# One layer's first adaLN modulation on four column tiles of the matmul engine, with the first group's r and k streamed after the opening

## The chip, the cores and the metric

The kernel runs on one core of a Trainium2 chip. A core has TensorE (PE, matmuls; PEld is its weight load), VectorE (DVE), ScalarE (ACT), GpSimd (POOL) and SyncE (SP), whose queue issues all the transfers here. The metric is the time of one execution on the device in microseconds; less is better.

## The reference, cut to what matters

Two layers of a decoder with 256 tokens and width 2048, all in fp32. Each layer modulates its input by six vectors made from one conditioning vector, projects it, runs two head groups, and then a SwiGLU.

```python
cond = jax.nn.silu(c)
for l in range(DEPTH):
    mod = (jnp.einsum('bd,de->be', cond, w_ada[l]) + b_ada[l]).reshape(B, N_MOD, 1, D_MODEL)
    sh_m, sc_m, gt_m, sh_f, sc_f, gt_f = [mod[:, i] for i in range(N_MOD)]
    u = x * (1 + sc_m) + sh_m
    proj = u @ w_in[l]
    ...   # sliding-window attention on q, k, v; RWKV-7 on r, k, v and the lora columns
    mix = jnp.concatenate([y_attn, y_rwkv], axis=-1) @ w_out[l]
    x = layer_norm(DEEPNORM_ALPHA * x + gt_m * mix, ln1_w[l], ln1_b[l])
    u = x * (1 + sc_f) + sh_f
    gate, up = jnp.split(u @ w_gate_up[l], 2, axis=-1)
    ffn = (jax.nn.silu(gate) * up) @ w_down[l]
    x = layer_norm(DEEPNORM_ALPHA * x + gt_f * ffn, ln2_w[l], ln2_b[l])
```

`w_ada[l]` is 2048 x 12288, so the two modulations that the first `u` needs (shift and scale, columns 0 to 4095 of layer 0) are 33.5 MB of weights for a product with a single row.

## The kernel before, in words

Weights stream from memory in raw tiles (`steps`): ScalarE rounds a tile to fp32r (`hi`, L380), VectorE takes the rest (`lo`, L381), and TensorE makes three fp32r products of each block (hi with u's high half, hi with its low half, lo with the high half; L414 to L416 in `tstream`, where u is the moving operand with 256 columns, L402 to L405 in `stream`). There are four raw tiles, three of hi and two of lo.

The opening is the part up to the first mixer. It goes over the 16 blocks of 128 columns of u in five parts of 4, 4, 2, 4 and 2 blocks (`PARTS`). For each part `ada_first` loads the weights of both modulations, 16 blocks of 128 rows, into tiles `ast`; VectorE multiplies each by its element of `cond` and adds it to `aacc` (L304, L306), which leaves one partial sum for each partition. `ada_sums` transposes the 128x128 blocks of `aacc` on TensorE (L277), ScalarE adds up along the free axis while it reads (L281), and VectorE adds the bias (L284). Then `make_u` transposes x (L354) and writes u's blocks (ScalarE L358, L360, VectorE L361). With every part of u that is ready, `front` runs three streams of columns: the 288 lora columns (`lb`), the 1024 of V (`acc`), and, with `ahead`, 384 columns of r and k: both r blocks and the first k block of group 0 (`rk`, and a third of it in `lb`). They accumulate in PSUM over all parts. A block of u takes 9 lora products, 9 of r and k, and 24 of V, and 42 in all.

The mixer works through groups in a fixed order (`ORDER`: D0 R0 A0 D1 R1 I0 ...). D0 makes the decays from the lora columns (products zb and ab, then vt from V), R0 (`project(0)`) streams the one k block that is left, A0 (`prepare`) mixes r and k with the token before (`shift_mix`, ScalarE and VectorE) and makes the chunk matrices, whose inversion I0 starts on TensorE at L749, after a round trip through memory and GpSimd.

The order on each engine is not that of the code: a scheduler sets it at build time from its own estimates. Each engine then works in that order and waits for semaphores. In PSUM the opening has bank m0 for all small work (transposes) and bank m1 for `rk`.

The remaining modulations run later, one load and one VectorE sum at a time beside the weight streams (`ada_steps`, L257).

## Time and profile before

| | us |
|---|---|
| time, median of 3 runs (lowest, highest) | 2701.08 (2698.25, 2703.82) |
| span of the profiled execution | 2692.6 |
| its granted TensorE clock, mean | 0.965 of full |
| TensorE busy over the span | 2501.1 |
| VectorE busy | 1841.0 |
| ScalarE busy | 1188.3 |
| first lora product of part 4 | 141.0 |
| last product of the opening's V stream | 177.3 |
| first product of R0 | 184.5 |

The profiled execution has no time of its own beside its span; the 8.5 us between its span and the runs' median stand for what lies around a span. A row of the profile gives the line, the engine, the operation, out<-in by the program's names, the shapes, and for groups the count, the busy time with the mean in ns, and the idle time ahead with what ended it. Rows of the timeline begin with the start and the length in us. Matmuls are pipelined: the distance of two starts is their price, not the length of one. An fp32 product stands in the trace as two passes, each with a weight load.

### The profile page before, as it was taken

The numbers are of one execution on the slowest core, as the hardware profiler recorded it, in microseconds if no ns is written. First come the engines' busy times: TensorE is split into PE (matmuls) and PEld (weight loads), VectorE is DVE, ScalarE is ACT, GpSimd is POOL, SyncE is SP. The second block draws the span as 40 slices with busy tenths as digits, with TensorE's granted clock in tenths as the row PEclk, the third lists the DMA queues.
The fourth block names the chain that finished last, engine by engine and source line by source line (L and its number), as shares of the span: only waits on it lengthen the run. The fifth ranks groups of instructions, "written<-read, shape, count | busy, mean of one in ns | idle before, by whom it ended". The sixth has DMA issues, their size and how long they took to land.

```text
span 2692.6 us, 41752 instructions
## 1 busy us (share of the span) xinstructions
PE 2501.1 (93%) x15325; PEld 2093.1 (78%) x15325; DVE 1841.0 (68%) x2469; ACT 1188.3 (44%) x2029; POOL 135.0 (5%) x355
## 2 busy tenths in 40 slices
PE   3788998788999999999999999979899999999997
PEld 2687886567888888888889877867688888888887
DVE  6866767979877777777788677555764545545456
ACT  2364452435444444444445544534444444344442
POOL 1002112000000000000000022110000000000000
PEclk9789998899999999999999999989999999999999
DMA  9968668688998888889878586424756656666654
GB/s 315 381 188 253 198 191 238 180 317 296 353 330 309 297 303 312 293 295 308 308 263 304 174 259 188 117 72 144 253 172 188 190 186 196 195 189 189 193 188 149
DMA packets 351999, 637.49 MB, mean 237 GB/s; under 512 B 75894, under 2 KB 142898, under 8 KB 350258
## 3 DMA queue, kind: packets, MB, share of 16 engines
q1 hardware_dynamic: 351794, 634.82, 71.6%
q8 instruction: 120, 1.97, 0.3%
q14 instruction: 85, 0.70, 0.1%
HBM read 622.08 MB, written 12.62 MB: 236 GB/s over the span
## 4 chain that ended last, share of the span: by engine, by line
PE 68%; DMA 8%; DVE 6%; ACT 2%; issue 1%; POOL 1%; SPq 0%; DVEq 0%; POOLq 0%; ACTq 0%
PE acc L403 19%; PE acc L402 19%; PE acc L405 19%; DMA ast<-in_w_ada_dram 3%; DVE aacc L257 2%; PE acc L414 2%; PE acc L415 2%; PE acc L416 2%; DVE lo L381 1%; DMA raw<-in_w_gate_up_dram 1%; PE mb L1225 1%; DMA raw<-in_w_out_dram 1%; DMA yf<-yd 1%; PE mb L277 1%; ACT pr L947 0%
## 5 line engine op out<-in xcount | busy, mean ns | idle before, releaser
L380 ACT CAST hi<-raw 128x1024 fp32r<-128x1024 f32 (+2 forms) x728 | 758.5, 1044 | 1110.8 <-PE acc L405 833.1
L381 DVE TENSOR_TENSOR lo<-raw,hi 128x1024 fp32r<-128x1024 f32 (+2 forms) x728 | 880.2, 1212 | 519.8 <-PE acc L403 347.1
L403 PE MATMUL acc<-lo,u 128*128 128x512 f32 x1568 | 513.4, 395 | 11.9 <-DVE lo L381 11.8
L405 PE MATMUL acc<-hi,u 128*128 128x512 f32 x1568 | 505.8, 391 | 0.0
L257 DVE SCALAR_TENSOR_TENSOR aacc<-ast,cond,aacc 128x1024 f32<-128x1024 f32 x300 | 384.1, 1280 | 127.8 <-DMA ast<-in_w_ada_dram 126.6
L402 PE MATMUL acc<-hi,u 128*128 128x512 f32 x1568 | 457.2, 393 | 0.9 <-ACT u L360 0.5
L403 PEld LDWEIGHTS acc<-lo,u 128*128 128x128 f32 x1568 | 293.8, 189 | 76.4 <-DVE lo L381 16.2
L402 PEld LDWEIGHTS acc<-hi,u 128*128 128x128 f32 x1568 | 294.9, 188 | 63.4 <-ACT sg L1218 0.9
L405 PEld LDWEIGHTS acc<-hi,u 128*128 128x128 f32 x1568 | 295.2, 188 | 61.8 <-issue 0.5
L403 PE MATMUL acc<-lo,ht 128*128 128x512 f32 (+1 forms) x720 | 243.6, 377 | 3.0 <-DVE lo L381 2.9
L405 PE MATMUL acc<-hi,ht 128*128 128x512 f32 (+1 forms) x720 | 242.2, 375 | 0.0
L414 PE MATMUL acc<-u,hi 128*128 128x256 f32 x720 | 206.1, 293 | 14.0 <-ACT hi L380 14.0
L402 PE MATMUL acc<-hi,ht 128*128 128x512 f32 (+1 forms) x720 | 217.0, 376 | 0.0
L415 PE MATMUL acc<-u,hi 128*128 128x256 f32 x720 | 204.5, 291 | 0.0
L416 PE MATMUL acc<-u,lo 128*128 128x256 f32 x720 | 193.1, 294 | 7.1 <-DVE lo L381 7.1
L403 PEld LDWEIGHTS acc<-lo,ht 128*128 128x128 f32 x720 | 135.0, 188 | 29.3 <-DVE lo L381 5.6
L414 PEld LDWEIGHTS acc<-u,hi 128*128 128x128 f32 x720 | 141.9, 197 | 19.3 <-ACT hi L380 14.9
L405 PEld LDWEIGHTS acc<-hi,ht 128*128 128x128 f32 x720 | 135.6, 188 | 24.2
L402 PEld LDWEIGHTS acc<-hi,ht 128*128 128x128 f32 x720 | 134.8, 188 | 24.4
L415 PEld LDWEIGHTS acc<-u,hi 128*128 128x128 f32 x720 | 141.7, 197 | 2.6 <-issue 1.6
L416 PEld LDWEIGHTS acc<-u,lo 128*128 128x128 f32 x720 | 133.8, 197 | 11.6 <-DVE lo L381 9.0
L1067 POOL TENSOR_TENSOR brs<-brs,mhalf 128x1 f32<-128x1 f32 x8 | 7.6, 955 | 1698.7 <-DVE brs L1066 772.1
(349 smaller groups left out, 2901.1 us busy)
## 6 DMA issues: line engine op xcount, KB each, us to landing
ast<-in_w_ada_dram SPq DMA_DIRECT2D x368, 512.0 KB
raw<-in_w_gate_up_dram SPq DMA_DIRECT2D x704, 256.0 KB
raw<-in_w_down_dram SPq DMA_DIRECT2D x176, 512.0 KB
raw<-in_w_in_dram SPq DMA_DIRECT2D x82, 512.0 KB
raw<-in_w_out_dram SPq DMA_DIRECT2D x64, 512.0 KB
raw<-in_w_in_dram SPq DMA_DIRECT2D x120, 256.0 KB
ast<-in_w_ada_dram SPq DMA_DIRECT2D x32, 256.0 KB
lnw<-in_ln_w_dram SPq DMA_DIRECT2D x4, 1024.0 KB
```

The source lines that it names most:

```text
L257: ins = V.scalar_tensor_tensor(acc, t, cond[:, j:j + 1], acc, ALU.mult, ALU.add)
L277: PE.transpose(b[:, i * P:(i + 1) * P], blocks[q + i], ident)
L380: S.copy(h, fl)
L381: ins = V.tensor_tensor(r, fl, h.bitcast(F32), ALU.subtract)
L402: PE.matmul(bt, lhsT=xh, rhs=hi[:, c0:c0 + w], start=st, stop=False)
L403: PE.matmul(bt, lhsT=xh, rhs=lo[:, c0:c0 + w], start=False, stop=False)
L405: PE.matmul(banks[t][q][:, 0:w], lhsT=xl, rhs=hi[:, c0:c0 + w], start=False, stop=sp_)
L414: PE.matmul(bt, lhsT=hi[:, c0:c0 + w], rhs=xh, start=st and opens, stop=False)
L415: PE.matmul(bt, lhsT=hi[:, c0:c0 + w], rhs=xl, start=False, stop=False)
L416: PE.matmul(bt, lhsT=lo[:, c0:c0 + w], rhs=xh, start=False, stop=sp_ and closes)
L1067: G.tensor_tensor(rs[:, 0:1], rs[:, 0:1], mhalf[:, 0:1], ALU.pow)
L1225: PE.transpose(b[:, i * T + t * P:i * T + (t + 1) * P], hh[t][:, (2 * k2 + i) * P:(2 * k2 + i + 1) * P], ident)
```

## The change

`ada_first` keeps its loads, but the product with `cond` is made by TensorE: for each block of 128 rows four fp32 products, one for each half of the two modulations' columns, on the four column tiles of 32 columns (`gv[32q:32q+32]`). The stationary operand is the element of `cond`, repeated 32 times, and the weights are the moving operand. They accumulate over the 16 row blocks in bank m1. ScalarE copies the result, TensorE transposes one or two 128x128 blocks, and VectorE adds the bias and the one of the scale. There are ten `ast` tiles instead of eight.

Bank m1 is thereby taken, and `front` loses `ahead`: R0 streams r and k of group 0 whole, as of the other groups, and its four shift mixes stand in `prepare`. The parameter rows, among them the bias, are transposed in two pieces (`par_block`), the first as soon as its rows are there. Line numbers move: L380, L381 become L391, L392; L414 to L416 become L425 to L427; L358, L360 become L369, L371; L354 becomes L365; L598, L599, L620 become L584, L585, L606; L749 becomes L732.

```diff
--- before.py
+++ after.py
@@ -166,6 +166,11 @@
     def drv(l, nm, i, n=1):
         return der[l][:, DO[nm] + i:DO[nm] + i + n]
 
+    def par_block(prow, l, i):
+        pt = bank()
+        PE.transpose(pt[:, 0:P], prow[:, i, :], ident)
+        V.tensor_copy(par[l][:, i, :], pt[:, 0:P])
+
     def setup(sp, l):
 
         prow = sp.tile([P, 2, P], F32, tag="prow", bufs=1, name=f"prow{l}")
@@ -176,6 +181,7 @@
             PC[nm] = r
             r += n
             yield
+        par_block(prow, l, 0)
         r = 0
         lst = [("ln2_w", ln2_w[l], 16), ("ln2_b", ln2_b[l], 16), ("w0", rwkv_w0[l], 8),
                ("a0", rwkv_a0[l], 8), ("k_k", rwkv_k_k[l], 8), ("k_a", rwkv_k_a[l], 8),
@@ -194,10 +200,7 @@
         dma(nsink[l], attn_sinks[l:l + 1, :].to_broadcast([P, 16]))
         V.tensor_scalar_mul(nsink[l], nsink[l], -1.0)
         yield
-        pt = bank()
-        for i in range(2):
-            PE.transpose(pt[:, i * P:(i + 1) * P], prow[:, i, :], ident)
-        V.tensor_copy(par[l].rearrange("p a b -> p (a b)"), pt[:, 0:2 * P])
+        par_block(prow, l, 1)
         V.tensor_scalar(drv(l, "omu", 0, 27), prm(l, "mu", 0, 27), -1.0, 1.0, ALU.mult, ALU.add)
         V.tensor_scalar_mul(drv(l, "w0h", 0, 8), prm(l, "w0", 0, 8), 0.5)
         V.tensor_scalar_mul(drv(l, "a0h", 0, 8), prm(l, "a0", 0, 8), 0.5)
@@ -293,20 +296,28 @@
     def ada_first(pool, c0, w):
 
         src = w_ada[0].rearrange("(j p) (m n) -> p j m n", p=P, m=6)
-        acc = pool.tile([P, 2, 512], F32, tag="aacc", name="aacc", bufs=2)[:, :, 0:w]
-        jj = 512 // w
+        jj, hw = 512 // w, w // 2
+        gv = ps.tile([P, 512], F32, tag="m1", name="gv", bufs=1)
         for j0 in range(0, KT, jj):
-            t = pool.tile([P, jj, 2, w], F32, tag="ast", name="ast", bufs=8)
+            t = pool.tile([P, jj, 2, w], F32, tag="ast", name="ast", bufs=10)
             for j in range(jj):
                 dma(t[:, j], src[:, j0 + j, 0:2, c0:c0 + w])
             for j in range(jj):
-                if j0 + j == 0:
-                    V.tensor_scalar_mul(acc, t[:, j], cond[:, 0:1])
-                else:
-                    V.scalar_tensor_tensor(acc, t[:, j], cond[:, j0 + j:j0 + j + 1], acc, ALU.mult, ALU.add)
+                for q in range(4):
+                    PE.matmul(gv[32 * q:32 * q + 32, 0:hw], lhsT=cond[:, j0 + j:j0 + j + 1].to_broadcast([P, 32]),
+                              rhs=t[:, j, q // 2, q % 2 * hw:q % 2 * hw + hw], start=(j0 + j == 0), stop=(j0 + j == KT - 1))
             yield
+        row = pool.tile([P, 256], F32, tag="arow", name="grow", bufs=2)
+        S.copy(row[:, 0:hw], gv[:, 0:hw])
+        b = bank()
+        for i in range(hw // P):
+            PE.transpose(b[:, i * P:(i + 1) * P], row[:, i * P:(i + 1) * P], ident)
+        n = w // P
+        bv = b[:, 0:hw].rearrange("p (i q r) -> p q i r", q=4, r=32)
         for m in range(2):
-            ada_sums(0, m, c0, [acc[:, m, i * P:(i + 1) * P] for i in range(w // P)])
+            col = m * KT + c0 // P
+            V.scalar_tensor_tensor(mods[0][:, col:col + n].rearrange("p (q i) -> p q i", q=2), bv[:, 2 * m:2 * m + 2, :, 0],
+                                   float(m), prm(0, "b_ada", col, n).rearrange("p (q i) -> p q i", q=2), ALU.add, ALU.add)
 
     done = set()
 
@@ -460,32 +471,18 @@
         V.tensor_tensor(yl[:, 1, :], y, yl[:, 0, :].bitcast(F32), ALU.subtract)
         return yl
 
-    def front(l, us, feeds, ahead=False):
+    def front(l, us, feeds):
 
         lb = [bank("lb", "cb") for _ in range(2)]
         vb = [acc_ps.tile([P, 512], F32, tag="acc", name="acc") for _ in range(4)]
         lblocks = [(0, 128, lb[0][:, 0:T], True, False), (128, 128, lb[0][:, T:2 * T], False, True),
-                   (256, 32, lb[1][0:32, 0:T], not ahead, not ahead)]
+                   (256, 32, lb[1][0:32, 0:T], True, True)]
         vblocks = [((2 * q + i) * P, P, vb[q][:, i * T:(i + 1) * T], i == 0, i == 1) for q in range(4) for i in range(2)]
-        rk = None
-        if ahead:
-            b = ps.tile([P, 512], F32, tag="m1", name="rk0", bufs=1)
-            turn[:] = 0, 0
-            rk = [[b[:, 0:T], b[:, T:2 * T]], [lb[1][:, T:2 * T], None]]
-            rblocks = [(0, P, rk[0][0], True, False), (P, P, rk[1][0], True, True), (2 * P, P, rk[0][1], False, True)]
-            wrk = w_in[l][:, R0:R0 + 2 * RW].rearrange("(k p) (s n) -> p k s n", p=P, s=2)
-
-            def rk_cols(rv, k0, m):
-                return [(rv[:, :, 0:T], wrk[:, k0:k0 + m, 0, 0:T]), (rv[:, :, T:T + P], wrk[:, k0:k0 + m, 1, 0:P])]
         for kts, _ in feeds:
             fl = dict(first=kts[0] == 0, last=kts[-1] == KT - 1)
-            if ahead and kts[0] == 0:
-                tstream(rk_cols, T + P, kts, us, rblocks, **fl)
             tstream(cols(w_in[l], LORA0, 288), 288, kts, us, lblocks, **fl)
-            if ahead and kts[0] > 0:
-                tstream(rk_cols, T + P, kts, us, rblocks, **fl)
             tstream(cols(w_in[l], R0 + 2 * RW, RW), RW, kts, us, vblocks, **fl)
-        return lb, vb, rk
+        return lb, vb
 
     def mixer(l, us, mixp, feeds):
 
@@ -494,13 +491,7 @@
         pa_cm = tc.tile_pool(name=f"pre{l}", bufs=1, reuse_waits="tile")
         pa = pa_cm.__enter__()
 
-        lb, vb, rk = feeds
-        x0 = {}
-        if rk:
-            for i, s in ((0, 1), (0, 0), (1, 0)):
-                x0[i, s] = pa.tile([P, T], F32, tag=("t_xr", "t_xk")[s], name="x0", bufs=(2, 4)[s])
-                shift_mix(l, x0[i, s], rk[i][s], 8 * s + i)
-            turn[1] = 1
+        lb, vb = feeds
 
 
         xwa = pa.tile([P, T], F32, name="xwa")
@@ -574,11 +565,6 @@
         KH = BH[::-1]
 
         def project(g):
-            if g == 0 and rk:
-                b = acc_ps.tile([P, 512], F32, tag="acc", name="acc")
-                c0 = R0 + RW + P
-                tstream(cols(w_in[l], c0, P), P, list(range(KT)), us, [(0, P, b[:, T:2 * T], True, True)])
-                return [None, b]
             bk = [acc_ps.tile([P, 512], F32, tag="acc", name="acc") for _ in I2]
 
             def rk_cols(rv, k0, m):
@@ -630,11 +616,8 @@
             for i in I2:
                 s_, p = st[i], 2 * g + i
                 for s, nm in ((1, "xk"), (0, "xr")):
-                    if g == 0 and (i, s) in x0:
-                        s_[nm] = x0[i, s]
-                    else:
-                        s_[nm] = pa.tile([P, T], F32, tag=f"t_{nm}", name=nm, bufs=(2, 4)[s])
-                        shift_mix(l, s_[nm], bk[i][:, s * T:(s + 1) * T], 8 * s + p)
+                    s_[nm] = pa.tile([P, T], F32, tag=f"t_{nm}", name=nm, bufs=(2, 4)[s])
+                    shift_mix(l, s_[nm], bk[i][:, s * T:(s + 1) * T], 8 * s + p)
             ssb = bank("ssb")
             for i in I2:
                 kkn = pa.tile([P, T], F32, tag="t_kkn", name="kkn", bufs=2)
@@ -1311,7 +1294,9 @@
             G.memset(zt, 0.0)
             for t in tinv:
                 dma(t.rearrange("e s t -> (e s t)").rearrange("(p n) -> p n", p=P), zt)
-        feeds = front(0, us, parts(), ahead=True)
+        turn[:] = 0, 0
+        feeds = front(0, us, parts())
+        turn[1] = 1
     for l in range(L):
         pace[0] = AP[l]
         with tc.tile_pool(name=f"mix{l}", bufs=1, reuse_waits="tile") as mp:
```

VectorE, from the end of part 3 to the end of part 4 of the opening, before. `aacc` is the sum for the modulation, `lo` the low half of a raw tile, `mods` the finished modulation:

```order
L381 TENSOR_TENSOR lo<-raw,hi 128x768
L306 SCALAR_TENSOR_TENSOR aacc<-ast,cond,aacc 128x1024 x5
L381 TENSOR_TENSOR lo<-raw,hi 128x1024 x2
L306 SCALAR_TENSOR_TENSOR aacc<-ast,cond,aacc 128x1024
L304 TENSOR_SCALAR aacc<-ast,cond 128x2x256
L306 SCALAR_TENSOR_TENSOR aacc<-ast,cond,aacc 128x2x256
L381 TENSOR_TENSOR lo<-raw,hi 128x864
L306 SCALAR_TENSOR_TENSOR aacc<-ast,cond,aacc 128x2x256 x2
L381 TENSOR_TENSOR lo<-raw,hi 128x288
L306 SCALAR_TENSOR_TENSOR aacc<-ast,cond,aacc 128x2x256 x2
L284 SCALAR_TENSOR_TENSOR mods_135<-asum,par_131 128x4
```

The same place now:

```order
L392 TENSOR_TENSOR lo<-raw,hi 128x576
L392 TENSOR_TENSOR lo<-raw,hi 128x1024 x2
L392 TENSOR_TENSOR lo<-raw,hi 128x864
L392 TENSOR_TENSOR lo<-raw,hi 128x288
L319 SCALAR_TENSOR_TENSOR mods_135<-mb,par_131 128x4 x2
L372 TENSOR_TENSOR u<-uf,u 128x256 x4
```

The sums between the low halves are gone, and nothing but low halves stands ahead of part 4's modulation.

TensorE, from the last V product ahead of part 4's modulation to part 4's first lora products, before (`mb` is a transpose, `acc` V, `lb` lora):

```order
L416 MATMUL acc<-u,lo 128x256
L277 MATMUL mb<-ident,aacc 128x128 x8
L354 MATMUL mb<-ident,xt 128x128 x4
L414 MATMUL lb<-u,hi 128x256
L414 MATMUL lb<-u,hi 32x256
```

The same place now:

```order
L427 MATMUL acc<-u,lo 128x256
L307 MATMUL gv<-ast,cond 32x256 x20
L314 MATMUL mb<-ident,grow 128x128 x2
L365 MATMUL mb<-ident,xt 128x128 x4
L307 MATMUL gv<-ast,cond 32x128 x12
L425 MATMUL lb<-u,hi 128x256
L425 MATMUL lb<-u,hi 32x256
```

In place of eight transposes stand the last twenty products of part 4's modulation, two transposes, and the first twelve of part 5's.

TensorE at the end of the opening and the start of R0, before (`zb`, `ab`, `vt` belong to D0, `ssb` to A0; the `acc` behind them is R0's k block):

```order
L416 MATMUL acc<-u,lo 128x256
L598 MATMUL zb<-twd,w2a_1668 128x256 x2
L599 MATMUL ab<-xwa,w2a_1668 128x256 x2
L620 MATMUL vt<-cent,vx 64x128
L644 MATMUL ssb<-bones,kkn 64x2 x4
L620 MATMUL vt<-cent,vx 64x128 x7
L414 MATMUL acc<-u,hi 128x256
```

The same place now:

```order
L427 MATMUL acc<-u,lo 128x256
L585 MATMUL ab<-xwa,w2a_1641 128x256 x2
L584 MATMUL zb<-twd,w2a_1641 128x256 x2
L606 MATMUL vt<-cent,vx 64x128 x8
L425 MATMUL acc<-u,hi 128x256
```

The products of A0 that stood between V and R0 stand after R0 now.

## The prediction

> **What bounds the kernel now.** I read the page's busy times and its chain of work first, then the opening in windows.
>
> ```profile
> span 2692.6 us, 41752 instructions
> ...
> PE 2501.1 (93%) x15325; PEld 2093.1 (78%) x15325; DVE 1841.0 (68%) x2469; ACT 1188.3 (44%) x2029; POOL 135.0 (5%) x355
> ...
> PE 68%; DMA 8%; DVE 6%; ACT 2%; issue 1%; POOL 1%; SPq 0%; DVEq 0%; POOLq 0%; ACTq 0%
> ```
>
> Over the whole span TensorE is the bound, so a product that is added or moved costs its full time unless it lands where TensorE idles. The opening is the place that the change touches. Its windows (busy times of PE, PEld, DVE, ACT, POOL, then granted clock, DMA share and GB/s):
>
> ```profile
> 75.00:100.00 25.00, 20.25 (x148) 18.65 (x148) 22.88 (x42) 12.85 (x35) 0.00 (x0) 0.86 1.07 375
> 100.00:125.00 25.00, 18.05 (x126) 16.91 (x124) 20.94 (x21) 8.25 (x14) 0.00 (x0) 0.86 1.05 394
> 125.00:150.00 25.00, 18.21 (x103) 16.78 (x104) 20.33 (x30) 10.87 (x33) 0.00 (x0) 0.73 0.71 237
> 150.00:175.00 25.00, 23.49 (x195) 22.99 (x194) 11.79 (x17) 12.45 (x22) 0.85 (x3) 1.00 0.61 175
> ```
>
> Until about 140 us the transfers are the limit (share 1.05 and more, 375 to 394 GB/s), VectorE is nearly full too, and TensorE has room. After that transfers fall to 0.61 and TensorE is dense: a tail of products that came too late. The tail on TensorE, and what VectorE did ahead of it (L306 is the sum for the modulation, L381 the low halves of the streamed weights):
>
> ```profile
> L306 DVE SCALAR_TENSOR_TENSOR aacc<-ast,cond,aacc 128x1024 f32<-128x1024 f32 (+1 forms) x75 | 80.2, 1069 | 12.1 <-DMA ast<-in_w_ada_dram 10.6
> 119.34 6.56 DVE L306 SCALAR_TENSOR_TENSOR aacc<-ast,cond,aacc 128x1024 f32<-128x1024 f32 x5
> 125.82 2.35 DVE L381 TENSOR_TENSOR lo<-raw,hi 128x1024 fp32r<-128x1024 f32 x2
> 128.09 1.28 DVE L306 SCALAR_TENSOR_TENSOR aacc<-ast,cond,aacc 128x1024 f32<-128x1024 f32 x1
> ```
> ```profile
> 134.61 0.60 PE L277 MATMUL mb<-ident,aacc 128*128 128x128 f32 x4
> ...
> 139.24 0.66 PE L354 MATMUL mb<-ident,xt 128*128 128x128 f32 x4 [1.72 <-ACT mb L281]
> 141.00 0.79 PE L414 MATMUL lb<-u,hi 128*128 128x256 f32 x2 [1.11 <-ACT u L360]
> ...
> 143.03 0.41 PE L416 MATMUL lb<-u,lo 128*128 128x256 f32 x1
> 143.25 0.41 PE L415 MATMUL lb<-u,hi 128*32 128x256 f32 x1
> 143.46 0.41 PE L416 MATMUL lb<-u,lo 128*32 128x256 f32 x1
> ...
> 159.82 0.28 PE L415 MATMUL acc<-u,hi 128*128 128x256 f32 x1
> 159.94 0.28 PE L414 MATMUL acc<-u,hi 128*128 128x256 f32 x1
> ...
> 167.08 0.50 PE L414 MATMUL lb<-u,hi 128*128 128x256 f32 x2 [1.50 <-ACT u L360]
> ...
> 177.34 0.28 PE L416 MATMUL acc<-u,lo 128*128 128x256 f32 x1
> 177.55 0.48 PE L598 MATMUL zb<-twd,w2a 64*128 64x256 f32 x1
> 177.57 0.48 PE L599 MATMUL ab<-xwa,w2a 64*128 64x256 f32 x1
> 177.87 0.38 PE L598 MATMUL zb<-twd,w2a 64*128 64x256 f32 x1
> 177.89 0.38 PE L599 MATMUL ab<-xwa,w2a 64*128 64x256 f32 x1
> ...
> 184.45 0.58 PE L414 MATMUL acc<-u,hi 128*128 128x256 f32 x1
> ```
>
> A streamed product of 256 columns starts every 0.12 us at the full clock (159.82, 159.94) and every 0.21 us at the half clock (143.03, 143.25). Part 4's modulation (blocks 10 to 13 of u) is summed at 129.4, its transposes wait behind V products until 134.6, and its first lora product starts at 141.0. V's last product starts at 177.34; the first group's own r, k stream starts at 184.45.
>
> **The change, part by part.** *Transfers.* Counted from the order in which SP issues them, the last weights of part 4's modulation stand behind 42.65 MB before and 41.13 MB now, those of part 5 behind 48.23 and 47.05 MB: the r, k pieces are gone, but V's come earlier. What the queue had moved in the profiled run by these times:
>
> ```profile
> 0.00:119.00 119.00, 59.78 (x388) 54.74 (x389) 89.56 (x136) 34.57 (x82) 9.78 (x63) 0.90 0.99 345
> 0.00:123.00 123.00, 63.45 (x417) 58.17 (x417) 93.49 (x139) 35.05 (x83) 9.78 (x63) 0.90 0.99 347
> 0.00:135.00 135.00, 72.58 (x469) 67.06 (x469) 103.54 (x150) 38.01 (x86) 9.78 (x63) 0.89 1.00 348
> 0.00:138.10 138.10, 73.44 (x473) 67.48 (x473) 106.50 (x155) 39.93 (x97) 9.78 (x63) 0.89 1.00 349
> ```
>
> 119 x 345 is 41.1 MB, 123 x 347 is 42.7, 135 x 348 is 47.0, 138.1 x 349 is 48.2. So part 4's weights land at 119 instead of 123 us, part 5's at 135 instead of 138.
>
> *The sum on VectorE* (80.2 us by L306) and the 32 transposes with their reductions go. None of it is on the path by itself, since the transfers cover it; what goes with it is the lag behind the landing: 123 to 129.4 in VectorE's order, and then 5.2 us in TensorE's, because the V products ahead had waited for low halves that stood behind five sums (119.34, then 125.82).
>
> *The product on TensorE.* For 48 steps of 256 columns and 32 of 128 there are four fp32 products each. One fp32 product is two passes: 256 columns take 0.21 us a pass (zb, 177.87 after 177.55, the first with its fill). Two column tiles run beside each other in this profile: eight products of 128 columns in the program, 16 passes, on two tiles of 64:
>
> ```profile
> 239.51 1.09 PE L620 MATMUL vt<-cent,vx 128*64 128x128 f32 x16
> ```
>
> One after another these 16 would take 1.7 us (0.107 each); they take 1.09 with the last one's drain. For four tiles the bounds of a 256-column step are 0.43 us (all beside each other) and 1.7 us (in turn). I take 0.43, since vt, the nearest row, overlaps fully. In all that is 64 x 0.43 = 28 us, at half clock 49; about 25 to 45 of it lies before 120 us, where it replaces 90 r, k products (10 blocks x 9, 11 to 19 us) in windows in which TensorE idles 5 to 7 us of 25 and the clock is granted at 0.86. Here I cost it at nothing; the cover is the transfers. If it is gone, TensorE's lag goes straight into the tail. A product that waits for its weights now stands in TensorE's order ahead of u's transposes and the V products; behind those wait the low halves, the raw tiles and SP:
>
> ```profile
> SPq L372 <- DVE lo L381: 65.1, 28, 11.4
> ```
>
> Walking through the order with the landing times above, each raw tile is free 2 to 10 us before SP needs it, so I take no bubble. The Trainium skill, TensorEngine Tiling (Array Packing), Key Properties, says that changing the tiling mode drains the engine; the trace steps from a 128x128 form to a 128x32 one in 0.22 us at half clock, the plain pitch (143.03 to 143.25), so the row speaks against a charge, and by the rule the sum would only grow.
>
> *The tail.* Part 4's last step is done at about 120.5 (119 and 1.5 for a step and the lag). Then come a copy of 128x256 (0.56, as L358), two transposes (0.4), two small VectorE sums (0.4), x's transposes (0.66), uf and u (1.12), and handovers; I put 4 us, where before 134.6 to 141.0 took 6.4 for eight reductions more:
>
> ```profile
> L358 ACT ACTIVATE uf<-mb,mods 128x256 f32<-128x256 f32 x16 | 9.0, 562 | 10.3 <-PE mb L354 10.3
> ```
>
> So the tail starts at 124.5 instead of 141.0. Before, 252 products (6 blocks x 42) took 36.3 us: 30.2 at full pitch, and 6.1 of half clock, transposes and one gap. Now there are 198 (6 x 33): 23.8, the same 6.1, 16 steps of 128 columns of part 5's modulation (16 x 0.21 = 3.4), and the gap before part 5 grows by 1.3, as its chain starts only when TensorE gets to the last 15 products: 34.6. V ends at 159 instead of 177.3: 18 us gained.
>
> *r, k of the first group.* The own stream grows from 48 to 192 products: 144 x 0.12 = 17.3 us, in a stretch where TensorE is the bound. The three shift mixes that stood between V's end and 184.45 leave that gap (ACT and VectorE 0.47 each; I take 1.5 us of the 7.1), and stand after the stream instead, on the chain to the inversion (1.4 us), which is late already:
>
> ```profile
> 247.59 0.50 PE L402 MATMUL acc<-hi,u 128*128 128x512 f32 x1
> 254.79 1.44 PE L749 MATMUL m<-ytr,am 64*64 64x64 f32 x22 [6.70 <-DVE ytr L745]
> ```
>
> The program puts the same TensorE work between the stream's end and this product as before, so the wait stays. The transfers moved here meet a queue at 0.61. Splitting the parameter transposes in two costs a VectorE copy, under transfers.
>
> Sum: -18 - 1.5 + 17.3 + 1.4 = -0.8; the spans of steps that I rounded upwards (the 4 us chain, the 6.1) make me take -2. The profiled execution's span is 2692.6, its time with what lies around it is taken as the median 2701.1, 8.5 us more: 2699.
>
> **The rivals.** *Only two tiles beside each other.* If matmuls start strictly in program order, a tile's second pass holds the next tile back, and a step costs 4 x 0.21 = 0.85 us. In the program both zb products stand ahead of both ab; the trace starts zb, ab, zb, ab, so it speaks against. Price: 3.4 us in the tail, 2 us in part 4's last steps: 2704. The Trainium skill, TensorE: Matmul & The Clock Gate, Part 3, has matmuls in strict FIFO, without reordering; by that rule this rival holds, and the zb and ab rows disagree with it.
>
> *TensorE's order stalls the opening.* One mechanism: products of the modulation wait at the head of TensorE for weights that land late, V's products wait behind, low halves and raw tiles are not freed, and SP, which waits 65.1 us on them already, holds the next weights back. Each lost microsecond of the queue moves V's end one for one; it decides from 6 us on, and with tiles in turn (64 x 1.7 = 109 us beside 63 for 528 front products) it would be 15 to 25. I put 2713. For it: TensorE's order follows estimates, not landings. Against: the walk above, and TensorE's idle time.
>
> *The opening shortens more.* The transfers aren't even in the first 60 us:
>
> ```profile
> 40.00:50.00 10.00, 0.00 (x0) 0.00 (x0) 5.12 (x4) 1.00 0.97 317
> 50.00:60.00 10.00, 0.00 (x0) 0.00 (x0) 5.12 (x4) 1.00 0.90 294
> ```
>
> With ten tiles in flight instead of eight and no 512-byte pieces of k, 375 GB/s there would give 4 us, and a TensorE that stays at the full clock another 4 to 6 in the tail: 2689.
>
> **How the numbers follow.** Forecast 2699, chance 0.50, by itself 2691 to 2706 (chain 3 to 5 us, clock in the tail, mixes); two tiles 0.15; stall 0.15; shorter opening 0.20. The range reaches to 2685 and 2716, which leaves out the worst of the stall and a gain over 16 us. A run tells 0.2% (5.4 us) from no change. Faster by more than that: 0.32 of the forecast, nearly all of the shorter opening, 0.37; slower: a fifth of the forecast, a third of two tiles, most of the stall, 0.28; the rest, 0.35, is within.
>
> **What the profile would show.** Right: the aacc rows of L306 are gone and VectorE is under half busy from 75 to 125 us; four products start within some 0.03 us of each other; the last weights land near 135; zb starts near 159 and the first group's r, k stream ends near 190. Wrong: DMA share well under 1 between 60 and 130 us; TensorE waiting for weights with V products behind; a step of 0.85 us or more at full clock; zb after 163; or a longer wait at the inversion's first product.

## The result, and the profile after

The changed kernel takes 2717.5 us (median of 4 runs, 2712.7 to 2720.4) and the kernel before 2701.4 us beside it (4 runs): a ratio of 1.007, 95% interval 1.0049 to 1.0092. It is slower by some 16 us, where 2699 was forecast and the range ended at 2716.

The page of the profiled execution after, with the lines that answer to those of before (span, busy times, shares of the chain that ended last):

```profile
span 2715.1 us, 42776 instructions
PE 2545.2 (94%) x15941; PEld 2101.6 (77%) x15941; DVE 1763.8 (65%) x2389; ACT 1179.0 (43%) x1968; POOL 125.8 (5%) x355
PE 32%; DVE 1%; DMA 1%; POOL 0%; ACT 0%; issue 0%; SPq 0%; DVEq 0%; POOLq 0%; ACTq 0%
```

VectorE lost 77 us of work and TensorE gained 44. The last line can't be laid beside that of before: the chain is followed back only to 1757 us here, so its shares add up to about a third of the span. The opening's windows, in the columns of before:

```profile
75.00:100.00 25.00, 24.00 (x253) 18.57 (x254) 8.30 (x20) 8.47 (x14) 0.00 (x0) 0.85 1.07 379
100.00:125.00 25.00, 22.52 (x243) 16.71 (x241) 6.03 (x11) 7.49 (x12) 0.00 (x0) 1.00 1.06 385
125.00:150.00 25.00, 23.77 (x261) 19.88 (x253) 8.81 (x12) 9.86 (x16) 0.14 (x1) 1.00 0.83 269
150.00:175.00 25.00, 20.39 (x137) 18.93 (x138) 12.06 (x23) 18.65 (x43) 1.09 (x5) 0.80 0.45 137
```

From 75 to 125 us VectorE is at a third or less, TensorE is nearly full (22.5 to 24.0 of 25 us in the first three windows), and the transfers still run at 1.06 and more: the products cost the queue nothing there. Rows of TensorE's timeline: a group of the modulation's products, the end of V's stream, and the first product of the inversion:

```profile
119.64 0.28 PE L427 MATMUL acc<-u,lo 128*128 128x256 f32 x1
119.84 1.50 PE L307 MATMUL gv<-ast,cond 128*32 128x256 f32 x24
...
160.22 0.28 PE L427 MATMUL acc<-u,lo 128*128 128x256 f32 x1
160.42 0.48 PE L585 MATMUL ab<-xwa,w2a 64*128 64x256 f32 x1
...
167.85 0.58 PE L425 MATMUL acc<-u,hi 128*128 128x256 f32 x1
...
253.06 0.28 PE L427 MATMUL acc<-u,lo 128*128 128x256 f32 x1
256.68 1.97 PE L732 MATMUL m<-ytr,am 64*64 64x64 f32 x32 [3.34 <-DVE ytr L728]
```

24 passes (three steps) take 1.50 us with the last one's drain, half a microsecond a step; the starts of two steps lie 0.43 us apart. V ends at 160.2 instead of 177.3, and the inversion's first product comes 1.9 us later than before (256.7 for 254.8) after a shorter wait (3.34 for 6.70). Up to here the change does about what was summed. The profiled span grew by 22.5 us, so nearly all of it lies behind this product. The medians stand only 16 us apart, because the profiled execution of before was a quick one: in the runs that have both, a time stands 1.6 to 2.1 us above its span, so of the 8.5 us that were put down to what lies around a span some 6 are this.

Windows by stage, from the opening's end to group 0's first product with its inverse (ta), to the end of the last q, k, v projection, and to the first product of the out projection (columns as above). Before:

```profile
177.55:278.90 101.35, 91.86 (x805) 81.18 (x806) 75.54 (x115) 53.90 (x108) 17.38 (x35) 0.93 0.77 239
278.90:423.30 144.40, 140.54 (x1432) 118.18 (x1429) 103.54 (x158) 69.67 (x139) 24.27 (x68) 1.00 0.67 203
423.30:530.70 107.40, 79.64 (x840) 61.38 (x838) 89.39 (x220) 43.29 (x156) 16.63 (x36) 0.79 0.69 198
```

After:

```profile
160.40:283.00 122.60, 114.61 (x1002) 103.98 (x1001) 91.20 (x134) 63.92 (x121) 13.06 (x35) 0.96 0.77 241
283.00:437.60 154.60, 141.11 (x1383) 116.18 (x1381) 104.98 (x155) 67.64 (x137) 28.70 (x68) 0.94 0.66 202
437.60:547.40 109.80, 76.21 (x830) 58.51 (x828) 83.24 (x213) 43.03 (x155) 12.76 (x36) 0.78 0.56 162
```

The kernel is 17.2 us ahead at the opening's end, 4.1 behind at 283, 14.3 behind when the projections end and 16.7 behind at the out projection. In the first two stages TensorE is busy 23.3 us longer (255.7 for 232.4; 17.3 was forecast for the moved products) and idle 8.1 longer (21.5 for 13.4). In the third it is idle some 28 to 34 us in both, and that stage is only 2.4 us longer.

The added idle time is in the second stage (3.9 us before, 13.5 after). TensorE's waits for low halves (`lo`) in it, before (278.9 to 423.3 us) and then after (283.0 to 437.6; us in all, times, longest):

```profile
PE acc L416 <- DVE lo L381: 2.6, 1, 2.6
PE acc L403 <- DVE lo L381: 0.9, 1, 0.9
```
```profile
PE acc L414 <- DVE lo L392: 6.8, 2, 4.4
PE acc L427 <- DVE lo L392: 4.9, 1, 4.9
```

That is 3.5 us before and 11.7 after; the section on the pull comes back to it.

One stall stands out, in the third stage. SP's timeline, a row of VectorE's and one of ScalarE's, and TensorE's wait between 430 and 475 us (us in all, times, longest), after:

```profile
444.44 1.31 SPq L710 DMA_DIRECT2D nb<-nscr  x2
457.91 1.27 SPq L721 DMA_DIRECT2D tinv<-ttl  x2
460.79 1.27 SPq L724 DMA_DIRECT2D tm<-tinv  x2
462.17 0.56 SPq L871 DMA_DIRECT2D qk<-qkv  x1
463.08 0.38 SPq L872 DMA_DIRECT2D qk<-qkv  x1
463.56 0.41 SPq L859 DMA_DIRECT2D qkv<-stg  x1
```
```profile
464.57 0.71 DVE L728 STREAM_TRANSPOSE ytr<-tm 128x512 f32<-128x512 f32 x1 [12.47 <-DMA tm<-tinv]
466.66 0.58 ACT L858 COPY stg<-acc 128x512 f32<-128x512 f32 x1 [12.87 <-DMA qkv<-stg]
```
```profile
PE ob L794 <- ACT state L813: 14.7, 3, 13.3
```

SP stands for 12 us at the last group's inversion (`tinv`), which GpSimd is still working out; behind it stand the attention's first loads (`qk`) and the store of a projected half (`qkv`). ScalarE's copy of the second half (L858) waits for that store, because both halves use one tile; behind the copy waits the state copy (L813), and behind that TensorE. The attention's first transposes start at 474.0 us instead of 452.6.

### The profile page after: what moved, and what is told of

Same layout as the page of the kernel before. It is cut to its first block, busy times and chain, and to the rows that moved or that the text cites. A ratio compares the mean times of both kernels' runs of the same rounds, so it can differ in the third digit from the quotient of the medians.

```text
span 2715.1 us, 42776 instructions
## 1 busy us (share of the span) xinstructions
PE 2545.2 (94%) x15941; PEld 2101.6 (77%) x15941; DVE 1763.8 (65%) x2389; ACT 1179.0 (43%) x1968; POOL 125.8 (5%) x355
## 5 line engine op out<-in xcount | busy, mean ns | idle before, releaser
L392 DVE TENSOR_TENSOR lo<-raw,hi 128x1024 fp32r<-128x1024 f32 (+2 forms) x726 | 879.5, 1214 | 569.8 <-PE acc L414 350.0
L391 ACT CAST hi<-raw 128x1024 fp32r<-128x1024 f32 (+2 forms) x726 | 758.0, 1047 | 1107.2 <-PE acc L416 843.6
L414 PE MATMUL acc<-lo,u 128*128 128x512 f32 x1568 | 515.0, 395 | 15.5 <-DVE lo L392 15.5
L416 PE MATMUL acc<-hi,u 128*128 128x512 f32 x1568 | 507.4, 393 | 0.0
L414 PEld LDWEIGHTS acc<-lo,u 128*128 128x128 f32 x1568 | 294.8, 189 | 79.6 <-DVE lo L392 18.7
L416 PEld LDWEIGHTS acc<-hi,u 128*128 128x128 f32 x1568 | 296.1, 189 | 62.0 <-issue 0.5
L414 PE MATMUL acc<-lo,ht 128*128 128x512 f32 (+1 forms) x720 | 243.6, 377 | 2.8 <-DVE lo L392 2.7
L416 PE MATMUL acc<-hi,ht 128*128 128x512 f32 (+1 forms) x720 | 242.2, 375 | 0.0
L425 PE MATMUL acc<-u,hi 128*128 128x256 f32 x768 | 218.2, 292 | 2.8 <-ACT hi L391 2.8
L426 PE MATMUL acc<-u,hi 128*128 128x256 f32 x768 | 217.5, 290 | 0.0
L427 PE MATMUL acc<-u,lo 128*128 128x256 f32 x768 | 205.8, 292 | 7.2 <-DVE lo L392 7.1
L414 PEld LDWEIGHTS acc<-lo,ht 128*128 128x128 f32 x720 | 135.1, 188 | 28.9 <-DVE lo L392 5.2
L425 PEld LDWEIGHTS acc<-u,hi 128*128 128x128 f32 x768 | 150.7, 197 | 7.9 <-ACT hi L391 3.7
L416 PEld LDWEIGHTS acc<-hi,ht 128*128 128x128 f32 x720 | 135.6, 188 | 24.2
L427 PEld LDWEIGHTS acc<-u,lo 128*128 128x128 f32 x768 | 142.1, 195 | 14.2 <-DVE lo L392 9.3
L426 PEld LDWEIGHTS acc<-u,hi 128*128 128x128 f32 x768 | 150.5, 197 | 1.9 <-issue 1.0
```

What stands on the lines that cost most here:

```text
L391: S.copy(h, fl)
L392: ins = V.tensor_tensor(r, fl, h.bitcast(F32), ALU.subtract)
L414: PE.matmul(bt, lhsT=xh, rhs=lo[:, c0:c0 + w], start=False, stop=False)
L416: PE.matmul(banks[t][q][:, 0:w], lhsT=xl, rhs=hi[:, c0:c0 + w], start=False, stop=sp_)
L425: PE.matmul(bt, lhsT=hi[:, c0:c0 + w], rhs=xh, start=st and opens, stop=False)
L426: PE.matmul(bt, lhsT=hi[:, c0:c0 + w], rhs=xl, start=False, stop=False)
```

## The experiments

Ratios are to the kernel before on the same chip; its median lay between 2691.8 and 2701.4 us in the sets of runs, so ratios, not times, are compared. Theory 1 said that the opening and the first group trade evenly and the re-timed order loses the time; rival 1, that r and k behind the opening are the loss; rival 2, that the products cost TensorE; rival 3, that a mended wait only moves. Theory 2, formed on the way, is told under the pull.

### The halves of the change

**r and k follow, the modulation stays on VectorE.**

```diff
-feeds = front(0, us, parts(), ahead=True)
+feeds = front(0, us, parts())
```

> Kernel before with half of the change: modulation still VectorE sums, but r and k of the first group follow the opening. Rival 1 (moving r and k is the loss): 2713 to 2719, with TensorE's first inversion product late by 8 us or more. Theory 1: the opening loses about as much weight as the first group gains in products, so the first inversion product stands within 5 us of before's 254.8; the time is what the re-timed order makes of it, 2696 to 2712, and any loss lies in waits of TensorE after 290 us.

Ratio 1.0069 (1.0044 to 1.0095), 2715.1 us: the whole loss, with the same 13.5 us stall at 454.0 us. The inversion's first product stands at 258.0. (Without `ahead`, bank m1 also serves the transposes of this opening.)

**Product modulation, r and k stay in the opening** (`gv` in bank m0, the parameter transposes moved behind its copy, `ahead` kept).

```diff
+gv = ps.tile([P, 512], F32, tag="m0", name="gv", bufs=1)
...
 feeds = front(0, us, parts(), ahead=True)
```

> The other half of the change: the opening's modulation as four column tiles of products, its sums in the bank that the transposes use, while r and k of the first group stay in the opening as before. Theory 1: the opening's last weights land up to 4 us earlier than in the kernel before, the rest is as before: 2695 to 2703, if the order later carries no new stall. Rival 1: the same. Rival 2 (the products on TensorE themselves cost the time): 2708 to 2718, with the end of V's products later than before's 177.6 us.

Ratio 1.0008 (0.999 to 1.0027): no change. V's end comes at 180.5 us, 3 later than before, which rival 2 had named, but without its price. The products aren't the loss, and by themselves are no gain either. What is lost comes with r and k.

### The stall

**The store on ScalarE's queue**, in the kernel after and, as control, before.

```diff
-dma(qkv[l, t, :, c0:c0 + 512], sg)
+S.dma_start(qkv[l, t, :, c0:c0 + 512], sg)
```

> Kernel after with one edit: the store of each projected q, k, v half stands on ScalarE's own queue, right behind the copy that fills its tile, instead of on SP's, where the store of 463.6 us stood behind the round trip of an inversion. Theory 1 (opening and first group are a wash; the loss is the re-timed order, above all the 13.5 us in which TensorE waits for the state copy behind the blocked tile): that wait goes, 2702 to 2708 us. Rival 1 (r and k of the first group behind the opening are themselves the loss): 2714 to 2719, as after. Rival 3 (the inversion's chain is the real bound, and the wait only moves): 2712 to 2718, with a wait of about 10 us for the inversion's results in the place of this one.

> Kernel before with the same edit as the run ahead of it, as its control. The two waits of the tile's copy there are 6.7 us together and TensorE's idle stretch beside them 8.5 us. Theory 1: a gain of 0 to 7 us, 2694 to 2702, so that the two kernels with this edit stand within 8 us of each other. Rival 1: the same 2694 to 2702 here, but 14 us or more between the two.

1.0072 (1.0047 to 1.0097) and 0.9989 (0.9974 to 1.0005). The edit moved the wait and did not end it: the copy of the second half now runs at 455.3 us, but its store, on ScalarE's queue, goes out only at 468.9, and the state copy stands behind it. What the trace names is the attention's load, which stands on SP; why the store waits for that load no run shows. ScalarE's wait in this run (430 to 475 us):

```profile
ACT state L813 <- DMA qk<-qkv: 13.4, 1, 13.4
```

**A second tile for the projected half.**

```diff
-sg = (pt or pa).tile([P, 512], F32, tag="stg", name="stg", bufs=1)
+sg = (pt or pa).tile([P, 512], F32, tag="stg", name="stg", bufs=2 if pt else 1)
```

> Kernel after with a second buffer for the tile of the projected halves, where the attention's pool is open (the third projection). So ScalarE's copy of the second half no longer waits for the first half's store, which itself still stands on SP behind the inversion. Theory 1 in its first form (the blocked copy is the loss): TensorE's 13.5 us stretch at 455 to 468 us goes, 2703 to 2708 us. Theory 1 in its second form (SP's queue is the loss: it stands 15 us at 443 to 458 for GpSimd's last inversion step, and the loads of the attention stand behind it as well as the store): the stall at the state copy goes, but the attention's first transposes still start near 474 us, and the time falls by 0 to 6 us only, 2711 to 2718. Rival 1 (r and k behind the opening are the loss by themselves): 2714 to 2719, with no long wait of TensorE left between 450 and 500 us.

1.0078 (1.0061 to 1.0095), no gain. TensorE's wait for the state copy is down to 1.9 us, and the 13 us are there again in the waits of TensorE, at the next consumer of the same queue:

```profile
PE acc L889 <- DVE qr L882: 12.8, 1, 12.8
PE ob L794 <- ACT state L813: 1.9, 2, 1.0
```

**The inversion's transfers on GpSimd**, in the kernel after, in the kernel before, and in the one with product modulation and r, k in the opening.

```diff
-dma(diagonal(tz, 2, q), tt[64 * q:64 * q + 64])
+G.dma_start(diagonal(tz, 2, q), tt[64 * q:64 * q + 64])
...
-dma(tm[BH[i]], tz[8 * i:8 * i + 8, 0:CH].rearrange("e s t -> s e t"))
+G.dma_start(tm[BH[i]], tz[8 * i:8 * i + 8, 0:CH].rearrange("e s t -> s e t"))
```

> Kernel after with the four transfers of each inversion (its result to memory, and back) issued by GpSimd, which computes it, instead of by SP. Nothing on SP's queue then stands behind an inversion. Theory 1, second form: the 15 us in which no weight, no store and no attention load is issued go, TensorE loses 13.5 us of idle time, and the time falls to 2696 to 2706 us. Rival 1: 2712 to 2719. Rival 3 (the inversion's round trip itself bounds the mixer): 2712 to 2720, or slower where GpSimd's queue issues more slowly.

> Kernel before with the same edit, as control of the run ahead of it. There SP's longest wait for GpSimd's inversion is 8.6 us in three times and the loads of the attention stand ahead of it. Theory 1, second form: 2690 to 2698 us here, and within 6 us of the kernel after with this edit. Rival 1: the same here, and 14 us or more less than the kernel after with this edit.

> The product modulation with r and k kept in the opening (its run above: 2698.4 us, no change from before) together with the inversion's transfers on GpSimd. If the two are independent: that run plus what the edit gives the kernel before, 2690 to 2700 us. A version that beats both kernels would show here.

1.0052 (1.0037 to 1.0068), 1.0035 (1.0018 to 1.0052), 0.9993 (0.9983 to 1.0003). In the first the attention's transposes come back to 455 us, and still the out projection starts at 552: the edit has costs of its own, as the control shows (slower by 7.5 us, where a gain was forecast), and the two kernels stand 8.5 us apart. None of the forecasts for the first was met.

**The order alone.** In layer 0 the last inversion's transfers to memory are held, in the order alone, behind the third projection's last store and the last of the first attention loads.

```diff
+for nm in last:
+    tc.add_manual_dep(ins.ins, nm, order, reason="behind the attention's loads")
```

> Kernel after, with one constraint for the order: in layer 0 the last inversion's transfers to memory stand on SP behind the third projection's stores and the first attention loads, as in the kernel before, not ahead of them. Theory 1, second form (SP's queue is the loss): the attention's first transposes come at about 453 instead of 474 us, the 13.5 us idle stretch of TensorE goes, and the time falls by 8 to 16 us, to a ratio of 1.001 to 1.004. Rival 3 (the stretch is bound by something else and the wait only moves): ratio 1.005 to 1.008.

> The same constraint on the kernel with VectorE modulation and r, k behind the opening (ratio 1.0069 in its run, with the same idle stretch of 13.5 us at 454 us). Theory 1, second form: 1.000 to 1.004. Rival 3: 1.005 to 1.008.

1.0078 (1.0065 to 1.0091) and 1.0044 (1.0029 to 1.006, against 1.0069 without it). The 13.5 us stretch is gone in both and the transposes start at 462 and 460 us. With product modulation that gains nothing; with VectorE's some 7 us, but the intervals overlap. In the traces the third stage does get shorter (103.7 us for 109.8, and 104.2 for 116.0), but with product modulation the projections end at 443.1 us instead of 437.6, so that the out projection starts at 546.7, where it started at 547.4. In the kernel after the most visible stall was thus worth next to nothing: what the new order gained there it had lost ahead of it.

### How much follows the moved work

**One tile of three back in the opening.**

```diff
+if ahead and kts[0] == 0:
+    tstream(cols(w_in[l], R0 + RW, P), P, kts, us, [(0, P, rk, True, True)], **fl)
```

> Kernel after, with one of the three moved tiles of r and k (the first k tile, 48 products of 0.12 us and 1 MB of weights) back in the opening, in the half bank that is free there. Rival 1 (the loss goes with the moved work, some 19 us for 144 products): a third of it back, 2709 to 2713. Theories 1 and 2 (fallout of the order, no proportion): between 2700 and 2719, with the time set by the waits for the weights' split after 300 us; opening 5 to 6 us longer, the first mixes as much shorter.

1.0101 (1.008 to 1.0121): slower, not a third back. Group 0's first product with its inverse starts at 277 us, ahead of before's 279, and all the loss lies behind. No proportion to the work moved; but the group's own stream, now 384 columns wide, still has 8 steps.

**Three tiles left out.** `project(0)` streams only the last k tile, and all four mixes read it.

> Kernel after, with three of the four r, k tiles of the first group left out of the program altogether (their mixes read the fourth tile's products), so that 144 products and 3 MB of weights are gone and the opening keeps its 17 us gain. If the opening's gain is real for all that follows, and the moved work costs what it takes (17.3 us) and some 8 us of idle time behind it: 2676 to 2690 us, 27 us or more under after. If what follows is bound by a chain that takes no notice of the opening's end (the later modulation, the loads): 2696 to 2706 us, not faster than before.

0.9999 (0.998 to 1.0017). Without 144 products, and with the opening's gain, the kernel is as fast as before. The stream is then back at 2 steps too, so the run takes away the pull that is told next together with the products. Its stages:

```profile
160.80:273.00 112.20, 103.19 (x889) 91.95 (x888) 85.27 (x128) 58.94 (x116) 14.44 (x35) 0.94 0.77 242
273.00:408.70 135.70, 131.09 (x1310) 108.41 (x1310) 92.39 (x146) 66.39 (x136) 25.62 (x68) 0.99 0.62 190
408.70:524.50 115.80, 82.14 (x872) 63.53 (x871) 92.24 (x222) 42.62 (x155) 16.34 (x36) 0.73 0.64 192
```

It is 14.6 us ahead at the projections' end (408.7 for 423.3) and only 6.2 at the out projection: the stage between took 115.8 us, 34 of them with TensorE idle. Here an earlier opening wasn't worth its length; some of it was waited away later.

### The pull

Each step of a weight stream pulls some steps of the later modulation (a load of 512 KB and a VectorE sum) into the order: 0.65 a step in layer 0's mixer.

```python
def pump():
    pace[1] += pace[0]
    while pace[1] >= 1.0:
        pace[1] -= 1.0
        next(ada_rest, None)
```

Before, group 0's own stream has 2 steps, so 1.3 pulls. After, it is 512 columns wide and has 8: 5.2 pulls. (The opening's streams pull nothing: the rate is set behind them.) That is part of the change, and no line of the diff names it. Theory 2 said that the pull brings sums of the later modulation to VectorE early, so that low halves come late and TensorE waits for them.

**The pull at a quarter, after; and with the transfers on GpSimd.**

```diff
+was = pace[0]
+if l == 0 and g == 0:
+    pace[0] = was / 4
 tstream(rk_cols, 512, list(range(KT)), us, ...)
+pace[0] = was
```

> Kernel after, with the first group's r, k stream pulling a quarter as many steps of the later modulation per step of weights (8 steps x 0.65 = 5.2 pulls become 1.3, what its 2 steps pulled in the kernel before). Theory 2 (the moved stream drags VectorE sums of the later modulation forward into a stretch where the split of the weights is late; TensorE waits 5 us at 318, 5 at 381 and 3 us at 403 us for that split, against 3 in all before): 5 to 10 us faster than after, 2707 to 2712. Rival 1 (the moved products are the loss): 2714 to 2719.

> Both edits on the kernel after: the inversion's transfers on GpSimd (its run: 2710.8 us) and the slower pull of the later modulation beside the first group's stream. If the two causes add: 2701 to 2706 us. If the pull is no cause: 2708 to 2713 us.

1.0059 (1.004 to 1.0078) and 1.0071 (1.0053 to 1.009). By time the first looks like the 10 us expected (2706.7), but the kernel before ran at 2691.8 beside it. By ratio it can't be told from the kernel after. Its trace shows what the slower pull does in layer 0:

```profile
162.90:291.20 128.30, 115.55 (x1003) 104.59 (x1002) 89.64 (x132) 63.96 (x121) 17.52 (x35) 0.95 0.73 227
291.20:431.70 140.50, 138.30 (x1388) 114.10 (x1388) 99.43 (x153) 67.52 (x137) 23.29 (x68) 1.00 0.66 202
431.70:538.70 107.00, 82.18 (x825) 61.80 (x823) 89.21 (x219) 43.05 (x156) 20.56 (x36) 0.74 0.66 196
```

The second stage takes 140.5 us instead of 154.6, the 13.5 us stall is gone without any edit to SP's queue, and the out projection starts at 538.8: 8.7 us earlier than after, 8.0 later than before. The first stage is longer than after, 128.3 us for 122.6.

**On one chip: the kernel after, no pull in it, four times the pull in the kernel before, and the slow pull with VectorE's modulation.**

```diff
-pace[0] = was / 4
+pace[0] = 0.0          # after, no pull
...
+pace[0] = was * 4      # before, in its 2 steps
...
+pace[0] = was / 4      # VectorE modulation, r and k following
```

> The kernel after once more, as the reference on the chip of the next three runs: 1.005 to 1.009 of the kernel before.

> Kernel before, with its 2 steps of the first group's stream pulling four times as many steps of the later modulation (2.6 each, so 5.2, as the 8 steps of the kernel after do). Theory 2 (the pull is the cause of half the loss): 5 to 10 us slower than before. Rival (what the slower pull gave the kernel after was the luck of another order, or the moved products are the whole loss): within 4 us of before.

> Kernel after, in which the first group's stream pulls no step of the later modulation at all. Theory 2: 7 to 12 us faster than after on the same chip. Rival: within 4 us of after.

> VectorE modulation with r and k behind the opening (19 us slower than before in its first run), and the first group's stream pulling a quarter as many steps, as in the kernel before. Theory 2: 7 to 12 us faster than that run against the same before, a ratio of 1.002 to 1.005. Rival: the ratio stays at 1.006 to 1.008.

1.0063 (1.0044 to 1.0082); 1.0033 (1.002 to 1.0047), slower; 1.0108 (1.0087 to 1.013), slower still, where theory 2 had it 7 to 12 us faster and its rival unchanged; and 1.0001 (0.9985 to 1.0018), better than theory 2's 1.002 to 1.005. The last is the main finding: r and k follow the opening, and nothing is lost. Its stages:

```profile
163.40:287.30 123.90, 113.78 (x1003) 103.17 (x1002) 90.11 (x131) 63.17 (x119) 17.00 (x35) 0.96 0.76 235
287.30:427.90 140.60, 138.42 (x1389) 114.11 (x1388) 99.17 (x152) 67.63 (x137) 23.08 (x68) 1.00 0.65 201
427.90:529.60 101.70, 77.64 (x825) 60.32 (x823) 87.32 (x216) 42.95 (x156) 16.62 (x35) 0.75 0.67 201
```

TensorE idles 12.3 us in the first two stages, as before (13.4), and the projections end 4.6 us later than before. The attention's transposes start at 451 us, and the out projection at 529.6, a microsecond earlier than before. The second stage of the kernel before with the fast pull, and TensorE's waits for low halves in that stage, first with the fast pull, then in the kernel with VectorE's modulation, r, k following and the slow pull:

```profile
276.72:431.62 154.90, 144.18 (x1403) 120.46 (x1402) 107.31 (x158) 68.38 (x139) 28.59 (x68) 0.94 0.66 205
```
```profile
PE acc L416 <- DVE lo L381: 6.2, 1, 6.2
PE acc L403 <- DVE lo L381: 2.4, 1, 2.4
```
```profile
PE acc L416 <- DVE lo L381: 1.7, 1, 1.7
```

This holds in every trace. In the nine with 5.2 pulls beside the first group's stream and the inversion's transfers on SP, TensorE waits 8.6 to 12.4 us for low halves in the second stage, which takes 152.3 to 157.4 us. In the ten with 1.3 pulls or none it waits 0 to 4.6 us, and the stage takes 135.7 to 146.6. (The kernel after with the transfers on GpSimd and 5.2 pulls has 5.0 and 146.5.) It is so with either modulation: for this stage theory 2 is borne out.

The windows of the modulation's sums alone (length; VectorE's busy time with the number of sums; clock, DMA share, GB/s), before:

```profile
160.00:216.00 56.00, 6.68 (x6) 0.94 0.67 202
...
440.00:540.00 100.00, 38.64 (x31) 0.80 0.66 191
```

After:

```profile
160.00:216.00 56.00, 12.30 (x10) 0.94 0.79 248
...
440.00:540.00 100.00, 31.88 (x26) 0.76 0.56 163
```

Before with the fast pull, and then VectorE's modulation with r, k following and the slow pull:

```profile
160.00:216.00 56.00, 12.77 (x10) 0.94 0.73 232
...
440.00:540.00 100.00, 36.17 (x29) 0.78 0.60 177
```
```profile
160.00:216.00 56.00, 7.69 (x6) 1.00 0.70 217
...
440.00:540.00 100.00, 41.24 (x33) 0.75 0.65 200
```

In these four the number of sums between 160 and 216 us follows the pull, 6 or 10. The kernel after with the slow pull has 4 there, and the one with three tiles left out 10, since its later streams start earlier. The number in the attention's stretch (31, 26, 29, 33) does not order the times: product modulation with r, k in the opening has 29 there and loses nothing.

**What is shown and what is open.** Shown: with VectorE's modulation the move of r and k costs 19 us with the pull it brings along, and nothing with the pull of before; that pull alone costs the kernel before 9 us; and in the traces it lengthens the second stage by 10 to 14 us with either modulation. Open: with product modulation, which is the change itself, the slower pull brought the out projection 8.7 us forward in its trace, but the time by 0 to 10 us only, not clear of noise, and no pull cost 12 more. So for the change itself the pull is shown as the cause of a part at most, and the rest of the 16 us has no cause that a run shows. With no pull, layer 0's out projection starts 11.0 us later than before, and layer 1's ends 34.7 us later (1958.7 for 1924.0), so most of that loss lies between the two. Which pairs of edits collide in the re-timed order I could not predict, and no run shows a rule for it. No version beat the kernel before clear of noise; the best are the store on ScalarE (0.9989) and the product modulation with r, k ahead and the inversion's transfers on GpSimd (0.9993).

## Why the prediction was wrong

*The opening: right.* V's end was put at 159 and came at 160.2, part 4's first lora product at 124.5 and came at 125.8; the transfers stayed at 1.06; VectorE's sums are gone from it. The rival of a stalled opening fell with the DMA share, that of an opening that shortens more with V's end.

*Four tiles beside each other: right.* A step was put at 0.43 us and takes that from start to start; in turn two by two, three steps would have taken 2.6 us, not 1.50. The four products of a step start 6 to 7 ns apart (5.498, 5.505, 5.511 and 5.518 us in the first step). The Trainium skill's strict FIFO (TensorE: Matmul & The Clock Gate, Part 3), read as holding the next tile back behind a second pass, disagrees with this trace. Whether the passes were put in that order before they reached TensorE, the trace doesn't show.

*A step between the kinds of product: put at nothing, small.* A modulation product behind a V product starts 0.21 us after it instead of 0.12 (119.635 to 119.844), in 14 of the 15 places in the opening, so some 1.3 us in all; the step back costs about as much. It isn't the change of tile: lora products step from the 128x128 form to the 128x32 one in 0.12 us (127.629 to 127.747), as the prediction had read at half the clock, and a modulation product behind a lora product of its own 128x32 form starts 0.21 us after it too (132.616 to 132.822). The Trainium skill, TensorEngine Tiling (Array Packing), Key Properties, states a drain on a change of tiling mode; these rows show no charge for one. What costs the 0.09 us is open.

*The gap before R0: wrong, small.* It was to shrink by 1.5 us. From the last decay product's start to R0's first it is 6.1 us before (178.32 to 184.45) and 6.7 after (161.19 to 167.85): the mixes taken out had been hidden by the decays' chain.

*R0 and the mixes: somewhat low.* 17.3 and 1.4 us were put; from zb's start to group 0's first chunk products it took 33.3 us before (177.55 to 210.9) and 54.8 after (160.4 to 215.2): 21.5 more, of which the gap above is 0.6, so 20.9 where 18.7 was put.

*The step that failed* is "r, k of the first group". It counted the products of the moved stream and its mixes, and not all that it issues: eight steps pull 5.2 steps of the later modulation where two pulled 1.3. The sum then stopped at the inversion with "The program puts the same TensorE work between the stream's end and this product as before, so the wait stays", and put nothing behind it. Up to there it came out about right (+1.9 us, the wait 3.4 us shorter). Behind it the kernel lost 12 us more to the projections' end, with TensorE waiting 11.7 us for low halves instead of 3.5, and stood 16.7 us behind at the out projection. The pull moves loads and sums, not TensorE work, and with them the order of SP and VectorE for the rest of the mixer. The runs put it at 9 us in the kernel before, and at 18 with the move and VectorE's modulation (1.0069 and 1.0001); forecast was nothing. For the change itself they show it in the second stage, 14 us there, of which 8.7 are left at the out projection; how much of the whole 16 us it is stays open. No rival named a later stage at all: each had its price in the opening.

## What to carry over

Where streams pull other work along by count, a stream that is moved or split differently moves that work too: count its steps before and after, not only its products and bytes. In a program whose order is set at build time, a local edit re-times everything behind it; here single numbers moved the time between 1.000 and 1.011, so a change is tried at two or three settings of the neighbouring pace before its price is believed. The longest wait in a trace may be worth little: take it away and see where it goes before it is called the loss.

## What the runs showed that was not expected

- Two orders that differ by one pull rate over eight steps stand 18 us apart (ratios 1.0069 and 1.0001). In the kernel after no pull at all was slower than the full pull (1.0108 for 1.0063).
- A store put on ScalarE's queue still waited 13.4 us, by the trace for a load on SP's queue.
- Four fp32 products on column tiles of 32 run fully beside each other. A step from a streamed product to one of them costs 0.09 us, and a step from the 128x128 form to the 128x32 one by itself nothing.
